# Three edits in an exact-split trunk layer: where the ring's places begin, where two staged operands land, and where two SiLUs stand

## The chip, the cores and the metric

The kernel runs on one core of a Trainium2 chip. The metric is the device time of one execution in microseconds (us). Three runs of the kernel before gave 2100.77, 2100.97 and 2095.59 us, so its median is 2100.77 us. A fourth execution was recorded by the hardware profiler; all rows come from that one.

## The reference

One decoder layer on a sequence of 512 positions with 2048 channels, in float32:

```python
hn = rms_norm(x, norm_mix_pre)
proj = hn @ w_in                       # q | k | v | gate_b | gate_c | hc, 1024 columns each
a = diff_attention(q, k, v, lam, rel_bias)             # 8 heads, causal
a = rms_norm(a, subln_gain) * (1.0 - lambda_init)
c = rms_norm(gate_b * short_conv(gate_c * hc, conv_w), conv_norm_gain)
mix = concat(a, c) @ w_out
x = x + rms_norm(mix, norm_mix_post)
hn = rms_norm(x, norm_ffn_pre)
f = (silu(hn @ w_gate) * (hn @ w_up)) @ w_down         # 5632 hidden columns
out = x + rms_norm(f, norm_ffn_post)
```

## The kernel before

**Products of split operands.** Every large product is made of float32 values that are split in two: ACT copies the value in a reduced type to `hi` (line 99), DVE subtracts that from the value and keeps the rest as `lo` (line 100). A product then takes three matmuls for each slice of 128 rows: hi·hi, hi·lo and lo·hi. These are lines 133, 134 and 135, so nearly all matmuls of the profile stand on those three lines, and the tile names tell the stages apart.

**Stages in order of time.** The v columns of the in-projection (to 113 us, banks `pv`); the q and k columns, the project stage (113 to 272 us, banks `pqk`, moving operands in `t_all` and `acts`); the column jobs of the convolution (to 590 us, banks `pc_h`, `pc_c`, `pc_b`, 512 columns a matmul), with the attention beside them; the out-projection (596 to 775 us, banks `po`, 512 columns); the gate and up projections in quartets (775 to 1648 us, banks `pa`, `pb`, `pd`); the down projection (to about 2060 us, banks `pd`); and the last pieces.

**Quartets.** A quartet q is 256 columns of one of the two FFN matrices: even q are gate, odd q are up, 44 in all. Its product of 2048 × 256 weights by 512 positions is done with seven half-size products in place of eight, in the manner of Strassen, numbered i = 1 to 7. Each is 8 slices × 3 matmuls = 24 matmuls of 256 columns. The weights of a product are sums or differences of blocks made by DVE (`combine`, lines 1015 to 1021) in the raw buffers `raw_q` (gate) or `post` and `pre` (up). The moving operand of products 1, 5, 2 and 3 is in the tensor `acts` (parts `ffn_hi` and `ffn_lo`), that of 7, 6 and 4 in the tiles x0 to x5. Most quartets run their products as 1, 5, 7, 2, 6, 3, 4 (`PLAIN`). The quartets 5, 7, 12 and 24 (`CLOSE`) run them as 1, 2, 5, 7, 6, 3, 4, and `in_turn` issues the first four matmuls of product 5 ahead of product 2.

**The ring.** A product's weights, `hi` and `lo`, stand side by side in one of four places of the tensor `ring_all`, taken in rotation (`ring_tile`). In the program as built `ring_all` begins at byte 196064 of each partition and a place is 8320 bytes behind the one before, so the four begin at bytes 480, 96, 224 and 352 within 512. `acts` begins at byte 416 within 512 and its slices step by 512; the x tiles begin at byte 32. The other stages use the same ring: as weights, or in the down projection and the out-projection as the moving operand.

**The first quartets.** The first four quartets (`HEAD`) run in another order: products (0,1), (1,1), (0,2), (1,2), (2,1), (3,1), (2,2), (3,2), then (0,5), (0,7), (0,3), (0,6), (0,4), then the rest of quartets 1, 2 and 3. Thirteen of their operands (`STAGED`) are split early, written to DRAM (`stg`) and read back by `prepare` through SP's DMA queue: the first two into the buffers with the tag `raw`, of which there are two, the third into `spare`, the others into ring places. At (0,3), seven matmuls of (0,6) are issued ahead. `load_quartet` (line 979) loads the raw weights of later quartets; those of even quartets go to the `raw` buffers.

**Gathering.** `gather` runs behind each product. From quartet 4 on, behind product 1 ACT copies half a bank to `q1` (line 1119), which must come before product 2 may add to that bank. Behind product 4 DVE writes the middle of the result (line 1140) and, in a gate quartet, ACT applies SiLU to the whole 128 × 1024 result (line 1142). `finish` multiplies it with the up quartet's result at the end of the next quartet. Each engine runs its instructions in the order in which they are issued.

Of the kernel before, what the change touches and what calls it, by code (L numbers as in the profile page):

```python
# [12 lines left out]
F32R = mybir.dt.float32r  # L13
AF = mybir.ActivationFunctionType
# [4 lines left out]
P = 128  # L19
D = 2048  # L20
# [35 lines left out]
def trunk(ctx: ExitStack, tc: tile.TileContext, a, out):  # L56
    nc = tc.nc
# [17 lines left out]
    high = ctx.enter_context(tc.tile_pool(name="high", bufs=1, side="right"))  # L75
# [5 lines left out]
        for o in (16, 144 + NT * KC * P, 0, 128 + NT * KC * P)  # L81
    )
    ring = [1]
    ring_all = high.tile([P, 4 * (D + 32)], F32R, name="ring_all")

    def ring_tile(n, m, shift=0):

        i = ring[0] = (ring[0] + 1) % 4
        return ring_all[:, (D + 32) * i + shift :][:, : n * m].rearrange("p (n m) -> p n m", n=n)

    ident = const.tile([P, P], F32, name="ident")
    make_identity(nc, ident)
# [5 lines left out]
    def split(hi, lo, src):  # L98
        first = nc.scalar.copy(hi, src)  # L99
        second = nc.vector.tensor_tensor(out=lo, in0=src, in1=hi.bitcast(F32), op=ALU.subtract)  # L100
        return first.ins, second.ins
# [13 lines left out]
    def ring_parts(raw, n, m):  # L115
        hi = ring_tile(n, m)
        lo = ring_tile(n, m)
        split(hi, lo, raw)
        return hi, lo
# [215 lines left out]
    tmp = {}  # L335
# [432 lines left out]
    def place(tag, dtype=F32, shape=(P, D)):  # L768
        count = late["count"] = late.get("count", 0) + 1
        name = f"{tag}_{count}"  # L770
        return late["mp" if tag[0] == "m" else "fp"].tile(list(shape), dtype, tag=tag, bufs=1, name=name)
# [175 lines left out]
    CLOSE, CLOSE_D = (5, 7, 12, 24), (2,)  # L947
# [9 lines left out]
    def slot(kind):  # L957

        tag, first, width, count = {
            "sg": ("m0", 0, 1024, 2), "s1": ("m1", 0, 1024, 1), "q1": ("m1", 1024, 256, 2), "u": ("m1", 1536, 256, 2),  # L960
            "q57": ("m2", 0, 512, 2), "r": ("m2", 1024, 1024, 1),
        }[kind]
        if ("tmp", tag) not in late:
            late["tmp", tag] = place(tag)
        k = slots[kind] = slots.get(kind, -1) + 1
        o = first + (k % count) * width
        return late["tmp", tag][:, o : o + width]
# [5 lines left out]
    def load_quartet(q):  # L973
        if q % 2 == 0:
            r = [wp.tile([P, 8, 256], F32, tag="raw", name=f"raw_q{q}_{i}") for i in range(2)]
        else:
            r = [place(n, F32, (P, 8, 256)) for n in ("post", "pre")]
        for i in range(2):
            nc.sync.dma_start(r[i], quartet_cols(q)[:, 8 * i : 8 * i + 8, :])
        raws[q] = r  # L980
# [28 lines left out]
    def combine(q, s):  # L1009

        (p11, p21), (p12, p22) = ((r[:, :, :P], r[:, :, P:]) for r in raws[q])
        if s == 1:
            t = slot("s1") if q else place("spare")[:, :1024]
            tmp["s1"] = t.rearrange("p (k m) -> p k m", k=8)
            nc.vector.tensor_add(tmp["s1"], p21, p22)
        elif s == 3:
            nc.vector.tensor_sub(p21, p11, p21)
        elif s == 2:
            nc.vector.tensor_sub(p21, p22, p21)
        else:  # L1020
            nc.vector.tensor_sub(p12, p12, p21)

    def source(q, i):

        if i in (1, 2) and 0 < q < HEAD:
            return heads_raw[q][:, 8 * (i - 1) : 8 * i, :]
        (p11, p21), (p12, p22) = ((r[:, :, :P], r[:, :, P:]) for r in raws[q])
        return {1: p11, 2: p12, 3: p12, 4: p22, 5: tmp.get("s1"), 6: p21, 7: p21}[i]

    def prepare(n):  # L1030

        if n >= len(order):
            return prepare_down(n - len(order))
        q, i = order[n]
        if (q, i) in STAGED:

            if n < 2:
                w = wp.tile([P, 16, P], F32R, tag="raw", name=f"w_{q}_{i}")
            elif n == 2:
                w = place("spare", F32R, (P, 16, P))  # L1040
            else:
                w = ring_tile(16, P)
            nc.sync.dma_start(w.rearrange("p k m -> p (k m)").bitcast(F32), stg[STAGED.index((q, i))])
            operands[n] = w.rearrange("p (a k) m -> p a k m", a=2)
        else:
            src = source(q, i)
            if i == 7 and q >= HEAD:
                combine(q, 3)
            if i == (3 if q == last_q else 6):
                combine(q, 2)  # L1050
            if i == 3:
                combine(q, 4)
            w = ring_tile(16, P).rearrange("p (a k) m -> p a k m", a=2)
            made[q, i] = split(w[:, 0], w[:, 1], src)
            operands[n] = w
        if i == 4:
            if q < last_q - 1:
                load_quartet(q + 2)
            elif q == last_q - 1:
                for j in (0, 1):  # L1060
                    load_block(0, j)
                load_block(0, 2)
            else:
                load_block(0, 3)
# [48 lines left out]
    def gather(n):  # L1113

        q, i = order[n]
        early, (c, up), pq = q < HEAD, quartets[q], psq[q]
        if i == (5 if early else 1):
            tmp["q1", q] = slot("q1")
            nc.scalar.copy(tmp["q1", q], pq["a"][:, :256])  # L1119
        if i == 7:  # L1120
            tmp["r", q] = slot("r") if up else slot("sg")
            if not up:
                tmp["sg", c] = tmp["r", q]
            q57 = tmp["q57", q] = slot("q57")
            nc.scalar.copy(q57, pq["b"])
            nc.vector.tensor_add(tmp["r", q][:, 768:], q57[:, :256], q57[:, 256:])
        if i == 6:
            u = tmp["u", q] = slot("u")
            nc.vector.tensor_add(u, pq["d"][:, 256:], tmp["q1", q])
            nc.vector.tensor_add(tmp["r", q][:, 768:], tmp["r", q][:, 768:], u)  # L1130
            if early:
                nc.vector.tensor_add(tmp["r", q][:, :256], pq["a"][:, 256:], tmp["q1", q])
            else:
                nc.scalar.copy(tmp["r", q][:, :256], pq["a"][:, :256])
        if i != 4:
            return
        u, r = tmp["u", q], tmp["r", q]
        mid = r[:, 256:768].rearrange("p (h n) -> p h n", h=2)
        b = pq["b"].rearrange("p (h n) -> p h n", h=2)
        nc.vector.tensor_tensor(out=mid, in0=b, in1=u[:, None, :].broadcast_to([P, 2, 256]), op=ALU.add)  # L1140
        if not up:
            nc.scalar.activation(r, r, AF.Silu)

# [54 lines left out]
    def load_block(s, j):  # L1200

        g, cb = s // 4, s % 4
        if g > 2:
            return
        if j in (1, 2):
            t = wp.tile([P, 8, 256], F32, tag="raw", name=f"raw_b{s}_{j}")
        else:
            t = place(turns[count_b[0] % 3], F32, (P, 8, 256))
            count_b[0] += 1
        e, half = ((0, 0), (0, 1), (1, 1), (1, 0))[j]  # L1210
        n = FIRST[g + 1] - FIRST[g]
        c0 = cb * 512 + half * 256
        rows = w_down.rearrange("(c e p) m -> p c e m", e=2, p=P)
        nc.sync.dma_start(t[:, :n, :], rows[:, FIRST[g] : FIRST[g + 1], e, c0 : c0 + 256])
        blocks[s, j] = t
# [33 lines left out]
    def prepare_down(n):  # L1249
        if n >= len(steps):  # L1250
            return
        g, cb, i, hf = steps[n]
        s = 4 * g + cb
        ks = pairs(g, hf)
        b11, b12, b22, b21 = (blocks[s, j][:, ks.start : ks.stop, :] if (s, j) in blocks else None for j in range(4))
        if i == 5:
            nc.vector.tensor_sub(b11, b12, b11)
        if i == 7:
            nc.vector.tensor_sub(b12, b22, b12)
        if i == 6:  # L1260
            nc.vector.tensor_sub(b11, b22, b11)
        if i == 4:
            nc.vector.tensor_sub(b21, b21, b11)
        src = {1: b11, 5: b11, 7: b12, 2: b21, 6: b11, 3: b22, 4: b21}[i]
        w = ring_tile(2 * len(ks), 256).rearrange("p (a k) m -> p a k m", a=2)
        made["down"] = split(w[:, 0], w[:, 1], src)
        operands_d[n] = w
        if hf == 1:
            if i == 7:
                load_block(s + 1, 1)  # L1270
            if i == (6 if s in CLOSE_D else 3):
                load_block(s + 1, 2)
            if i == 4:
                load_block(s + 1, 3)
                load_block(s + 2, 0)
# [61 lines left out]
    def ffn(_):  # L1337
        ready, ng = 7, len(order)
        for n in (5, 6):
            prepare(n)  # L1340
# [146 lines left out]
```

## Time and profile before

| | before |
|---|---|
| median of three runs | 2100.77 us (2095.59 to 2100.97) |
| the profiled execution, as a run | 2097.92 us |
| its span, first to last instruction | 2096.1 us |
| mean granted TensorE clock | 0.996 |
| PE busy | 2072.3 us, 99% |
| DVE busy | 1609.6 us, 77% |
| ACT busy | 958.8 us, 46% |
| moved by DMA | 358.57 MB, 171 GB/s on average |

The span is what the profile shows; the run's own time is 1.8 us longer. A row of the timeline has the start in us, the duration in us, the engine, the line, the operation, out<-in with the tile names (buffer numbers left out), and in brackets the idle time of the engine just before and what ended it. A row of groups ends with the count, then the busy time in us and the mean of one in ns, then the idle time before. A row of windows has the stretch, its length, then the busy time (and instructions) of PE, of the weight loads, of DVE, ACT and POOL, then the granted clock, the share of the DMA engines and GB/s; where the view is of SP alone the engines are left out. PE's matmuls overlap, so their rate is read from their starts, not from their durations.

### The profile page before, as it was taken

Reading aid. Unit: us, or ns where it says so; the run is one execution under the profiler, and the core shown is the slowest. Engines: PE = TensorE matmul, PEld = TensorE weight load, DVE = VectorE, ACT = ScalarE, POOL = GpSimd, SP = SyncE. Lnnn points to the kernel's source line nnn. Section 1 sums busy time; section 2 is a strip of 40 time slices with the busy share of each in tenths; the row PEclk is TensorE's granted clock in tenths of the full one; section 3 lists DMA queues with packets and bytes.
Section 4 is the critical chain, followed back from the end, with each engine's and each line's share of the span. In section 5 each row is a group of like instructions: output and inputs, shape, how many; then the busy total and the mean of one; then the engine's idle time right before and its main releaser. Section 6 shows DMA issues by size and latency. Waiting matters only on the chain.

```text
span 2096.1 us, 35907 instructions
## 1 busy us (share of the span) xinstructions
PE 2072.3 (99%) x15180; PEld 1957.8 (93%) x15180; DVE 1609.6 (77%) x2027; ACT 958.8 (46%) x1341; POOL 25.3 (1%) x51
## 2 busy tenths in 40 slices
PE   8999999999999999999999999999999999999998
PEld 6899988888888889999999999999999999999996
DVE  5777747777455478988888889888888777878887
ACT  4344446654334354445445445445544444333442
POOL 0000000000000000000000000000000000000000
PEclk9999999999999999999999999999999999999999
DMA  6444353331239867554544544545545946648354
GB/s 234 137 158 150 112 191 95 98 109 63 92 137 346 293 227 246 176 156 150 158 156 153 161 151 153 163 148 159 160 146 173 331 145 228 230 120 287 106 186 161
DMA packets 301618, 358.57 MB, mean 171 GB/s; under 512 B 11880, under 2 KB 261736, under 8 KB 295568
## 3 DMA queue, kind: packets, MB, share of 16 engines
q1 hardware_dynamic: 299856, 350.48, 50.8%
q10 hardware_dynamic: 1600, 5.79, 0.8%
q8 instruction: 119, 1.95, 0.4%
q14 instruction: 43, 0.35, 0.1%
HBM read 289.11 MB, written 69.75 MB: 171 GB/s over the span
## 4 chain that ended last, share of the span: by engine, by line
PE 92%; DVE 4%; DMA 2%; issue 1%; ACT 1%; SPq 0%; POOL 0%; DVEq 0%; POOLq 0%; ACTq 0%
PE pb L134 7%; PE pb L133 7%; PE pb L135 7%; PE pd L133 6%; PE pd L134 6%; PE pd L135 6%; PE pa L133 5%; PE pa L134 5%; PE pa L135 5%; PE po L134 3%; PE po L133 3%; PE po L135 3%; PE pv L134 1%; PE pv L135 1%; PE pv L133 1%; PE pc_h L135 1%
## 5 line engine op out<-in xcount | busy, mean ns | idle before, releaser
L99 ACT CAST ring_all<-raw_q 128x1024 fp32r<-128x1024 f32 x124 | 130.0, 1050 | 195.2 <-PE pb L134 79.6
L134 PE MATMUL pb<-x,ring_all 128*128 128x256 f32 x704 | 197.2, 280 | 0.0
L135 PE MATMUL pb<-x,ring_all 128*128 128x256 f32 x704 | 197.0, 280 | 0.0
L133 PE MATMUL pb<-x,ring_all 128*128 128x256 f32 x704 | 196.9, 280 | 0.0
L135 PE MATMUL pb<-acts,ring_all 128*128 128x256 f32 x704 | 195.5, 278 | 0.4 <-DVE ring_all L100 0.4
L133 PE MATMUL pb<-acts,ring_all 128*128 128x256 f32 x704 | 195.7, 278 | 0.0
L134 PE MATMUL pb<-acts,ring_all 128*128 128x256 f32 x704 | 195.5, 278 | 0.0
L133 PE MATMUL pa<-acts,ring_all 128*128 128x256 f32 x680 | 190.8, 281 | 2.0 <-ACT m L1119 2.0
L134 PE MATMUL pa<-acts,ring_all 128*128 128x256 f32 x680 | 189.9, 279 | 0.0
L135 PE MATMUL pa<-acts,ring_all 128*128 128x256 f32 x680 | 189.8, 279 | 0.0
L135 PE MATMUL pd<-ring_all,acts 128*128 128x256 f32 x640 | 179.1, 280 | 0.6 <-DMA acts<-hx 0.6
L133 PE MATMUL pd<-ring_all,acts 128*128 128x256 f32 x640 | 179.2, 280 | 0.0
L134 PE MATMUL pd<-ring_all,acts 128*128 128x256 f32 x640 | 179.2, 280 | 0.0
L99 ACT CAST ring_all<-pre 128x1024 fp32r<-128x1024 f32 (+1 forms) x106 | 105.0, 994 | 148.2 <-PE pb L134 78.1
L100 DVE TENSOR_TENSOR ring_all<-raw_q,ring_all 128x1024 fp32r<-128x1024 f32 x124 | 151.2, 1220 | 27.2 <-ACT ring_all L99 26.9
L100 DVE TENSOR_TENSOR ring_all<-pre,ring_all 128x1024 fp32r<-128x1024 f32 (+1 forms) x106 | 122.0, 1153 | 54.4 <-ACT ring_all L99 53.5
L99 ACT CAST ring_all<-post 128x1024 fp32r<-128x1024 f32 (+1 forms) x106 | 105.2, 993 | 102.9 <-PE pd L135 42.4
L100 DVE TENSOR_TENSOR ring_all<-post,ring_all 128x1024 fp32r<-128x1024 f32 (+1 forms) x106 | 121.7, 1148 | 21.7 <-ACT ring_all L99 21.4
L134 PE MATMUL pd<-ring_all,x 128*128 128x256 f32 x480 | 134.6, 280 | 0.2 <-DVE ring_all L100 0.2
L135 PE MATMUL pd<-ring_all,x 128*128 128x256 f32 x480 | 134.4, 280 | 0.0
L133 PE MATMUL pd<-ring_all,x 128*128 128x256 f32 x480 | 134.4, 280 | 0.0
L133 PEld LDWEIGHTS pb<-x,ring_all 128*128 128x128 f32 x704 | 133.3, 189 | 0.0
(343 smaller groups left out, 6515.3 us busy)
## 6 DMA issues: line engine op xcount, KB each, us to landing
raw_q<-in_w_gate SPq DMA_DIRECT2D x42, 1024.0 KB, 5.9
post<-in_w_up SPq DMA_DIRECT2D x22, 1024.0 KB, 5.2
pre<-in_w_up SPq DMA_DIRECT2D x22, 1024.0 KB, 5.1
hx<-spare SPq DMA_DIRECT2D x20, 896.0 KB, 7.8
hx<-m SPq DMA_DIRECT2D x20, 896.0 KB, 8.5
raw_o<-in_w_out SPq DMA_DIRECT2D x16, 1024.0 KB, 7.9
raw_b<-in_w_down SPq DMA_DIRECT2D x16, 896.0 KB, 5.7
acts<-hx SPq DMA_DIRECT2D x32, 448.0 KB, 8.7
```

What stands on the lines that cost most here:

```text
L99: first = nc.scalar.copy(hi, src)
L100: second = nc.vector.tensor_tensor(out=lo, in0=src, in1=hi.bitcast(F32), op=ALU.subtract)
L133: yield nc.tensor.matmul(o, lhsT=lhi, rhs=rhi, start=start, stop=False, **kw).ins
L134: yield nc.tensor.matmul(o, lhsT=lhi, rhs=rlo, start=False, stop=False, **kw).ins
L135: yield nc.tensor.matmul(o, lhsT=llo, rhs=rhi, start=False, stop=stop, **kw).ins
```

## The change

There are three edits. The first changes the stride of the ring from `D + 32` to `D` elements and moves its last two places by 128 elements, 512 bytes. The tensor is 512 bytes larger than before, and it and `acts` begin 512 bytes lower. In the program as built the four places begin at byte 480 within 512, all of them; `acts` (416) and the x tiles (32) keep their bytes within 512. The second sends the staged operands (0,7) and (0,6) to the `raw` buffers in place of ring places. The third issues the SiLU of a gate quartet behind the next quartet's copy to `q1` where the next quartet is in `CLOSE`; of these only 5 and 7 follow a gate quartet, so two SiLUs move, those of quartets 4 and 6.

```diff
-    ring_all = high.tile([P, 4 * (D + 32)], F32R, name="ring_all")
+    ring_all = high.tile([P, 4 * D + 256], F32R, name="ring_all")
...
-        return ring_all[:, (D + 32) * i + shift :][:, : n * m].rearrange("p (n m) -> p n m", n=n)
+        return ring_all[:, D * i + 128 * (i // 2) + shift :][:, : n * m].rearrange("p (n m) -> p n m", n=n)
...
-            if n < 2:
+
+            if n < 2 or (q, i) in ((0, 7), (0, 6)):
                 w = wp.tile([P, 16, P], F32R, tag="raw", name=f"w_{q}_{i}")
...
             tmp["q1", q] = slot("q1")
-            nc.scalar.copy(tmp["q1", q], pq["a"][:, :256])
+            copy = nc.scalar.copy(tmp["q1", q], pq["a"][:, :256])
+            if q in CLOSE and ("silu", q - 1) in tmp:
+                with tc.issue_after(copy.ins):
+                    tmp.pop(("silu", q - 1))()
...
         if not up:
-            nc.scalar.activation(r, r, AF.Silu)
+            silu = lambda: nc.scalar.activation(r, r, AF.Silu)
+            if q + 1 in CLOSE:
+
+                tmp["silu", q] = silu
+            else:
+                silu()
```

The diff moves later lines: the staged load of line 1043 is line 1044 after the change, the copy to `q1` of line 1119 is 1120, and the SiLU of line 1142 is 1146.

On SP's queue, at the staged loads of quartet 0 and the first raw loads of quartet 2, there stands before (`pre` is a raw load of quartet 1; the five loads to the ring are the operands (0,5), (0,7), (0,3), (0,6) and (0,4)):

```order
L979 DMA pre_6628<-in_w_up 128x8x256
L1043 DMA ring_all<-stg 128x2048 x5
L979 DMA raw_q_0_6758<-in_w_gate 128x8x256
L979 DMA raw_q_1_6759<-in_w_gate 128x8x256
L979 DMA post_6934<-in_w_up 128x8x256
```

and after the change:

```order
L979 DMA pre_6628<-in_w_up 128x8x256
L1044 DMA ring_all<-stg 128x2048
L1044 DMA w_7_6665<-stg 128x2048
L1044 DMA ring_all<-stg 128x2048
L1044 DMA w_6_6722<-stg 128x2048
L1044 DMA ring_all<-stg 128x2048
L979 DMA raw_q_0_6760<-in_w_gate 128x8x256
L979 DMA raw_q_1_6761<-in_w_gate 128x8x256
L979 DMA post_6936<-in_w_up 128x8x256
```

The order of the loads is the same; two of them go to the buffers `w_7` and `w_6`, which the two loads to `raw_q_0` and `raw_q_1` take over next. The ring places of all later operands shift by two.

On ACT, at the border between quartets 6 and 7, there stands before (the last copy to m from pa at line 1134 is that of quartet 6; `pa_7949` is the bank of quartet 7):

```order
L1134 COPY m_53_6786<-pa_7739 128x256
L99 CAST ring_all<-m_52_6755 128x1024
L99 CAST ring_all<-post_7651 128x1024
L1142 ACTIVATE m_53_6786<-m_53_6786 128x1024
L1119 COPY m_52_6755<-pa_7949 128x256
L99 CAST ring_all<-post_7651 128x1024
```

and after the change (the bank is `pa_7950`):

```order
L1138 COPY m_53_6788<-pa_7741 128x256
L99 CAST ring_all<-m_52_6757 128x1024
L99 CAST ring_all<-post_7653 128x1024
L1120 COPY m_52_6757<-pa_7950 128x256
L1146 ACTIVATE m_53_6788<-m_53_6788 128x1024
L99 CAST ring_all<-post_7653 128x1024
```

SiLU and copy have changed places, and nothing else moved there. At the border between quartets 4 and 5 the same two are exchanged.

## The prediction

> **What bounds the kernel now.** I read the page first, then the chain, PE's waits, and PE's timeline product by product.
>
> ```profile
> span 2096.1 us, 35907 instructions
> PE 2072.3 (99%) x15180; PEld 1957.8 (93%) x15180; DVE 1609.6 (77%) x2027; ACT 958.8 (46%) x1341; POOL 25.3 (1%) x51
> PE 92%; DVE 4%; DMA 2%; issue 1%; ACT 1%; SPq 0%; POOL 0%; DVEq 0%; POOLq 0%; ACTq 0%
> PE pd L133 <- DMA ring_all<-stg: 2.2, 1, 2.2
> PE pa L133 <- ACT m L1119: 2.0, 1, 2.0
> ```
>
> The matmuls set the end: PE is busy for 99% of the span and carries 92% of the chain. Little waiting is left, and two of the longest single waits are quoted because the change touches both: 2.2 us before a product of quartet 0 whose staged operand arrives late, and 2.0 us in quartet 7 behind the copy of line 1119. So only three things can move the end: these two waits, new waits, and the rate at which PE takes matmuls.
>
> The rate is not one number. The next rows are the first matmuls of successive products in two neighbouring gate/up quartets, 14 and 15; each product is 24 matmuls long and nothing stands between them.
>
> ```profile
> 1059.72 0.28 PE L133 MATMUL pa<-acts,ring_all 128*128 128x256 f32 x1
> 1062.55 0.28 PE L133 MATMUL pb<-acts,ring_all 128*128 128x256 f32 x1
> 1065.27 0.28 PE L133 MATMUL pb<-x,ring_all 128*128 128x256 f32 x1
> 1068.10 0.28 PE L133 MATMUL pa<-acts,ring_all 128*128 128x256 f32 x1
> 1070.84 0.28 PE L133 MATMUL pa<-x,ring_all 128*128 128x256 f32 x1
> 1073.68 0.28 PE L133 MATMUL pb<-acts,ring_all 128*128 128x256 f32 x1
> 1076.42 0.28 PE L133 MATMUL pb<-x,ring_all 128*128 128x256 f32 x1
> 1079.25 0.28 PE L133 MATMUL pa<-acts,ring_all 128*128 128x256 f32 x1
> 1081.99 0.28 PE L133 MATMUL pb<-acts,ring_all 128*128 128x256 f32 x1
> 1084.71 0.28 PE L133 MATMUL pb<-x,ring_all 128*128 128x256 f32 x1
> 1087.54 0.28 PE L133 MATMUL pa<-acts,ring_all 128*128 128x256 f32 x1
> ...
> 1098.85 0.28 PE L133 MATMUL pa<-acts,ring_all 128*128 128x256 f32 x1
> ```
>
> Subtract neighbours. The products of quartet 14 take 2.83, 2.72, 2.83, 2.74, 2.84, 2.74 and 2.83 us; quartet 15 takes 2.74, 2.72, 2.83, and then 11.31 us for its last four, 2.83 each. Same instruction, same shape, two paces: 24 matmuls in 2.73 us (114 ns each) or in 2.83 us (118 ns). Set beside them the ring place that each operand has in the program as built (its first byte within 512). Quartet 14 goes through 96, 224, 352, 480, 96, 224, 352, and quartet 15 through 480, 96, 224, 352, 480, 96, 224. Products whose moving operand is in `acts` (i = 1, 5, 2, 3; the tensor begins at byte 416 and its slices step by 512) are fast at 480 and 224 in four cases of four, and slow at 96 and 352 in three of four. Products that move an x tile (i = 7, 6, 4; byte 32) are slow at all four places. The two quartets last 39.13 us.
>
> The pattern is not that of one pair alone. These are groups of lines 133 and 134 over all quartets from 4 on (863 to 1640 us), and one of the down projection:
>
> ```profile
> L134 PE MATMUL pa<-acts,ring_all 128*128 128x256 f32 x632 | 176.6, 279 | 0.0
> L134 PE MATMUL pb<-acts,ring_all 128*128 128x256 f32 x635 | 176.2, 277 | 0.0
> L133 PE MATMUL pd<-ring_all,acts 128*128 128x256 f32 x640 | 179.2, 280 | 0.0
> ```
>
> A slow matmul lasts 281 ns in the records and a fast one 276. By the pair, i = 1 and 2 (pa) are fast in two cases of four and i = 5 and 3 (pb) in three of four; that would give means of 278.5 and 277.2, and the groups show 279 and 277.
>
> **The change, part by part.** *The places.* Now every place begins at 480, and `acts` and the x tiles keep their bytes. Each `acts` product then stands where it was fast, each x product where it was slow. Of the pair's 14 products, eight go to 2.73 and six stay at 2.83: 38.82 us, 0.31 less. There are 20 pairs from quartet 4 on: **−6.2 us**. The alternative is that the pace follows what ran before rather than the byte: the product at 1081.99 is fast at a slow byte, directly behind a fast one. Bounds: all fast, 39.13 − 14 × 2.73 = 0.91 a pair, −18; all slow, 14 × 2.83 = 39.62, 0.49 a pair, +9.8. I take the byte, for seven `acts` cases of eight and the group means.
>
> The Trainium skill, page "SBUF — State Buffer", section "Who interferes with whom", gives PE two independent read ports, one for the moving operand and one for the weights, and says that PE never waits on anyone. By that no byte of a place can matter and this term would be 0, not −6.2; the rows at 1062.55 (2.72 us) and 1065.27 (2.83 us) show two paces that go with the operands' places, so the trace does not agree, though it does not show why.
>
> The down projection takes its moving operand from the ring; at 280 ns it is nearly all slow although its products pass through all four places, so I take 0 for it. If one in five of its 3360 matmuls is fast now (280 against 281 and 276) and becomes slow, that is +3. The project stage and the stages with 512 columns are next.
>
> ```profile
> L133 PE MATMUL pqk_b<-t_all,ring_all 128*128 128x256 f32 x192 | 53.4, 278 | 0.0
> L133 PE MATMUL pc_b<-acts,ring_all 128*128 128x512 f32 x128 | 51.0, 398 | 0.0
> L133 PE MATMUL po<-ring_all,acts 128*128 128x512 f32 x224 | 88.0, 395 | 0.0
> 739.92 0.39 PE L133 MATMUL po<-x,acts 128*128 128x512 f32 x1
> 743.36 0.39 PE L133 MATMUL po<-x,acts 128*128 128x512 f32 x1
> 751.34 0.40 PE L133 MATMUL po<-x,acts 128*128 128x512 f32 x1
> 756.24 0.40 PE L133 MATMUL po<-x,acts 128*128 128x512 f32 x1
> ```
>
> In the project stage, the three lines of `pqk_b` on `t_all` (576 matmuls) have a mean of 278: all slow +1.7, all fast −1.2. With 512 columns, three matmuls (one of each line) take 0.688 us (five between 739.92 and 743.36) or 0.700 us (seven between 751.34 and 756.24). The column jobs have 3 × 128 such triples and the out-projection 224, so 608 in all; each moves by at most 12 ns, ±7.3, and half of that if they are mixed now, as the means of 395 to 398 suggest. I take 0 for both stages, since the rows do not say which byte is the better one there.
>
> *The SiLU behind the copy.* Quartets 5 and 7 issue four matmuls of product 5 ahead of product 2, so the copy of line 1119 has only those to hide in.
>
> ```profile
> 881.82 0.28 PE L133 MATMUL pb<-acts,ring_all 128*128 128x256 f32 x1
> 882.10 0.38 PE L133 MATMUL pa<-acts,ring_all 128*128 128x256 f32 x1
> 887.40 1.05 ACT L99 CAST ring_all<-post 128x1024 fp32r<-128x1024 f32 x1 [5.35 <-DVE post L1019]
> 921.24 0.28 PE L133 MATMUL pb<-acts,ring_all 128*128 128x256 f32 x1
> 923.49 0.50 PE L133 MATMUL pa<-acts,ring_all 128*128 128x256 f32 x1 [1.97 <-ACT m L1119]
> 922.12 1.06 ACT L1142 ACTIVATE m<-m 128x1024 f32<-128x1024 f32 x1 [2.38 <-DVE m L1140]
> 923.50:927.00 3.50, 3.50 (x17) 3.50 (x18) 3.47 (x4) 1.05 (x1) 0.00 (x0) 0.51 0.18 53
> ```
>
> In quartet 7 the SiLU waits for a sum on DVE until 922.12, and the copy stands behind it although ACT has been idle for 2.38 us. PE pauses 2.25 us between starts (921.24 to 923.49) where quartet 5, whose SiLU was done in time, pauses 0.28: −1.97. Behind the pause the granted clock is 0.51, and 17 matmuls take 3.50 us instead of 17 × 0.118 = 2.0: −1.5. Together **−3.5 us**. Nothing takes the pause's place: behind the copy the SiLU still starts at 922.12. In quartet 5 the copy gains nothing and the SiLU comes about 2 us later, but ACT then sits idle for 5.35 us before its next cast (887.40), which hides 1.06 us. If that cover were gone, the casts behind it would be 1.06 us late: bound +1.
>
> The Trainium skill, page "TensorE: Matmul & The Clock Gate", Part 1, puts the fall to half clock behind an idle window of about 3.4 us. By that a pause of 2.25 us would not cause the 0.51, those 1.5 us could stay and the sum would be 1.5 higher; the trace has the 0.51 right behind the pause, so here it is counted with it.
>
> *The two loads.* Operands 7 and 6 of quartet 0 now go to raw buffers that have long been free, so the load of 6 no longer waits for a ring place.
>
> ```profile
> 808.14 0.36 PE L133 MATMUL pd<-x,ring_all 128*128 128x256 f32 x1 [2.23 <-DMA ring_all<-stg]
> 804.00:807.00 3.00, 1.00 0.87 300
> raw_q<-in_w_gate SPq DMA_DIRECT2D x42, 1024.0 KB, 5.9
> raw_q<-in_w_gate SPq DMA_DIRECT2D x2, 1024.0 KB, 12.5
> 819.98 1.21 DVE L1015 TENSOR_TENSOR m<-raw_q,raw_q 128x1024 f32<-128x1024 f32 x1
> ```
>
> Product 6 waits 2.23 us for it. But the DMA engines are near full there (0.87 busy at 300 GB/s in the stretch that ends at the landing), and the bytes ahead of it in the queue are the same, so an earlier issue mostly makes it stand longer in the queue. What can be filled is 0.13 × 3.00: **−0.4 us**; bounds 0 and −2.2. In exchange quartet 2's two raw loads, next on SP's queue, wait for these buffers, the second until product 6 ends. Product 6 issues 7 matmuls, then product 3 its 24, then product 6 the rest: 48 × 0.118 = 5.7 us behind 808.14, so 813.8. With 5.9 us to landing it is there at 819.7, and DVE first needs it at 819.98: hidden, with 0.3 us to spare. I take 0. The two loads themselves took 12.5 us when they stood behind the staged ones; with that the second would come at 826.3, 6 us late, and DVE would be late by as much with everything queued behind: bound +6.
>
> **The sum.** −6.2 − 3.5 − 0.4 = −10.1. The profiled execution took 2097.92 us as a run, so 2087.8. It lies 2.9 below the median of the three runs (2100.77), which themselves reach from 2095.59 to 2100.97; the four have a mean of 2098.8, 0.9 above it, and with this I say **2088.7 us**.
>
> **The rivals.** *The byte decides nothing for the pace.* Against it stand seven of eight cases; for it stands that x products are slow at all places and that 1081.99 does not fit. Then −3.9 alone: 2098.8 − 3.9 = 2094.9. The rule quoted above from the Trainium skill (page "SBUF — State Buffer") would give this too.
>
> *The pace has a memory and locks slow.* x products, three in seven, are always slow, and four slow products in a row run at the end of quartet 15, an `acts` product on 352 and one on 96 among them. Today it is the change of place between products that brings the fast pace back (1065.27 to 1068.10 changes 352 for 480). With one byte for all, that trigger is gone; if it is needed, all products are slow: +9.8 in the quartets, +1.7 in the project stage, less 3.9: 2106.4.
>
> *Slower than before: the same lock in the 512-wide stages too.* The mechanism is the last one, its place the column jobs and the out-projection as well as the quartets; its price 2106.4 plus half of 7.3, so 2110. It becomes slower than before once the pace lost exceeds the 3.9 that the waits give, which is when two fifths of the 9.8 come.
>
> *The edit of the loads or of the SiLU does not do what it says* (the load lands no earlier, the copy finds ACT busy with something else): 2088.7 plus 0.4 or 3.5, 2089 to 2092, inside the first case's range.
>
> **How the numbers follow.** The forecast has 0.46, the byte without effect 0.28, the slow lock in the quartets 0.18, and in all stages 0.08. About 0.3% is what a measurement of this kernel can tell from no change: faster means below 2094.5, slower above 2107.1. The first case is faster but for 0.03; the second lies on the border, half and half; the third is half same, half slower with the bounds of the other stages (half, because +3 on the down projection or part of the +6 of quartet 2's loads carries it over); the fourth is slower but for 0.02. That gives 0.57 faster, 0.28 same, 0.15 slower. The range leaves out the fourth case, the upper edge of the third, and gains beyond 7 us in the unpriced stages: 2081 to 2107. The forecast's own range is 2083 to 2094.
>
> **What would show it.** In the profile after, each step has its row. The places: `acts` products in the gate/up quartets take 2.73 us and x products 2.83, and the groups of pa and pb on `acts` both have a mean of 276 to 277; a mean of 280 to 281 is the lock. The SiLU: no row of L1120 among PE's waits and a clock of 1.00 at that place. The loads: PE's wait for `stg` loads becomes one on a `w` tile, about 1.8 us long, and no new wait stands in quartet 2. The prediction is wrong if the pace in the down projection or the 512-wide stages moves by more than its bounds, or if x products become fast as well.

## The result, and the profile after

The changed kernel takes 2068.72 us, the median of four runs (2066.94 to 2071.81), against 2100.03 us for the kernel before on the same chip (four runs). The ratio is 0.9857 with a 95% interval of 0.9837 to 0.9876: 1.4% faster, some 30 us. The forecast was 2088.7 us with a range from 2081 to 2107. The direction was right, and the gain is three times the forecast's.

The page of the profile after, its first lines and the chain:

```profile
span 2070.0 us, 35911 instructions
PE 2046.8 (99%) x15180; PEld 1936.9 (94%) x15180; DVE 1607.4 (78%) x2027; ACT 958.6 (46%) x1341; POOL 26.0 (1%) x51
PE 89%; DVE 4%; DMA 4%; issue 1%; ACT 1%; POOL 0%; SPq 0%; DVEq 0%; POOLq 0%; ACTq 0%
```

PE's busy time fell by 25.5 us and the span by 26.1 us. So, on balance, nearly nothing of the gain is a wait that went: the same 15180 matmuls run faster. (The span's gain is smaller than that of the medians, because the profiled execution of after, 2071.81 us, is the slowest of its four runs.)

Where they run faster can be read from the first matmul of each stage in the two profiles:

| first matmul of | before, us | after, us | gained in the stage ahead of it, us |
|---|---|---|---|
| the project stage | 115.80 | 114.79 | 1.0 (v columns) |
| the column jobs | 272.37 | 273.09 | −1.7 (project) |
| the out-projection | 590.76 | 587.76 | 3.7 (columns) |
| quartet 0 | 775.24 | 770.36 | 1.9 (out-projection) |
| quartet 4 | 859.21 | 854.76 | −0.4 (quartets 0 to 3) |
| quartet 8 | 941.61 | 933.37 | 3.8 (with quartet 7's wait) |
| the down projection | 1646.67 | 1632.93 | 5.5 (quartets 8 to 43) |
| the last pieces | 2043.32 | 2017.21 | 12.4 (down projection) |

The largest step is the down projection, which the forecast had at 0. Two of its groups of after:

```profile
L134 PE MATMUL pd<-ring_all,acts 128*128 128x256 f32 x640 | 176.8, 276 | 0.0
L134 PE MATMUL pd<-ring_all,x 128*128 128x256 f32 x480 | 132.7, 277 | 0.3 <-DVE ring_all L100 0.3
```

Both had a mean of 280 before: the down projection went over from the slow pace to the fast one. The quartets did what the forecast said. Quartet 14 in the timeline of after, the first matmul of each product, and that of quartet 15:

```profile
1051.25 0.28 PE L133 MATMUL pa<-acts,ring_all 128*128 128x256 f32 x1
1053.98 0.28 PE L133 MATMUL pb<-acts,ring_all 128*128 128x256 f32 x1
1056.70 0.28 PE L133 MATMUL pb<-x,ring_all 128*128 128x256 f32 x1
1059.53 0.28 PE L133 MATMUL pa<-acts,ring_all 128*128 128x256 f32 x1
1062.25 0.28 PE L133 MATMUL pa<-x,ring_all 128*128 128x256 f32 x1
1065.08 0.28 PE L133 MATMUL pb<-acts,ring_all 128*128 128x256 f32 x1
1067.81 0.28 PE L133 MATMUL pb<-x,ring_all 128*128 128x256 f32 x1
1070.63 0.28 PE L133 MATMUL pa<-acts,ring_all 128*128 128x256 f32 x1
...
1090.01 0.28 PE L133 MATMUL pa<-acts,ring_all 128*128 128x256 f32 x1
```

All four `acts` products take 2.72 to 2.73 us, all three x products 2.82 to 2.83; the pair of quartets takes 38.76 us (forecast 38.82, before 39.13).

The waits of PE after, those that the change touches:

```profile
PE pd L135 <- DVE ring_all L100: 1.6, 2, 1.2
...
PE pd L133 <- DMA w<-stg: 0.4, 1, 0.4
...
PE pa L133 <- ACT m L1120: 0.3, 1, 0.3
```

The wait for product 6 of quartet 0 fell from 2.23 to 0.36 us; two waits of DVE's, 1.6 us together, are new. They are in quartets 2 and 3, and the timeline shows what they hang on (DVE first, then PE):

```profile
815.41 1.23 DVE L1015 TENSOR_TENSOR m<-raw_q,raw_q 128x1024 f32<-128x1024 f32 x1 [2.82 <-DMA raw_q<-in_w_gate]
```

```profile
801.82 0.36 PE L133 MATMUL pd<-x,w 128*128 128x256 f32 x1 [0.36 <-DMA w<-stg]
...
830.59 0.39 PE L135 MATMUL pd<-x,ring_all 128*128 128x256 f32 x1 [0.40 <-DVE ring_all L100]
...
846.41 0.38 PE L135 MATMUL pd<-x,ring_all 128*128 128x256 f32 x1 [1.21 <-DVE ring_all L100]
```

DVE stood still for 2.82 us until quartet 2's raw weights came, and its operands for quartets 2 and 3 were late by 0.40 and 1.21 us. The border between quartets 6 and 7, on ACT and in a window of all engines:

```profile
916.63 0.37 ACT L1120 COPY m<-pa 128x256 f32<-128x256 f32 x1 [1.08 <-PE pa L135]
917.93 1.06 ACT L1146 ACTIVATE m<-m 128x1024 f32<-128x1024 f32 x1 [0.93 <-DVE m L1144]
```

```profile
915.50:919.00 3.50, 3.49 (x31) 3.29 (x30) 3.47 (x5) 1.48 (x3) 0.00 (x0) 1.00 1.15 345
```

The copy now follows PE at once, and PE runs through: 31 matmuls in 3.5 us at a clock of 1.00.

### The profile page after: what moved, and what is told of

Read it like the earlier page. It is cut to its first block, busy times and chain, and to the rows that moved or that the text cites. A ratio compares the mean times of both kernels' runs of the same rounds, so it can differ in the third digit from the quotient of the medians.

```text
span 2070.0 us, 35911 instructions
## 1 busy us (share of the span) xinstructions
PE 2046.8 (99%) x15180; PEld 1936.9 (94%) x15180; DVE 1607.4 (78%) x2027; ACT 958.6 (46%) x1341; POOL 26.0 (1%) x51
## 4 chain that ended last, share of the span: by engine, by line
PE 89%; DVE 4%; DMA 4%; issue 1%; ACT 1%; POOL 0%; SPq 0%; DVEq 0%; POOLq 0%; ACTq 0%
PE pb L134 6%; PE pd L135 6%; PE pb L133 6%; PE pd L134 6%; PE pb L135 6%; PE pd L133 6%; PE pa L133 5%; PE pa L134 5%; PE pa L135 5%; PE po L135 3%; PE po L133 3%; PE po L134 3%; DVE ring_all L100 2%; DMA raw_q<-in_w_gate 2%; PE pv L134 1%; PE pqk_b L133 1%
## 5 line engine op out<-in xcount | busy, mean ns | idle before, releaser
L134 PE MATMUL pb<-x,ring_all 128*128 128x256 f32 x696 | 194.8, 280 | 0.0
L135 PE MATMUL pb<-x,ring_all 128*128 128x256 f32 x696 | 194.3, 279 | 0.5 <-DVE ring_all L100 0.5
L133 PE MATMUL pb<-x,ring_all 128*128 128x256 f32 x696 | 194.2, 279 | 0.0
L133 PE MATMUL pd<-ring_all,acts 128*128 128x256 f32 x640 | 176.9, 276 | 0.7 <-DMA acts<-hx 0.7
L135 PE MATMUL pd<-ring_all,acts 128*128 128x256 f32 x640 | 176.9, 276 | 0.7 <-DMA acts<-hx 0.7
L134 PE MATMUL pd<-ring_all,acts 128*128 128x256 f32 x640 | 176.8, 276 | 0.0
L134 PE MATMUL pd<-ring_all,x 128*128 128x256 f32 x480 | 132.7, 277 | 0.3 <-DVE ring_all L100 0.3
L133 PE MATMUL pd<-ring_all,x 128*128 128x256 f32 x480 | 132.6, 276 | 0.0
L135 PE MATMUL pd<-ring_all,x 128*128 128x256 f32 x480 | 132.6, 276 | 0.0
L135 PEld LDWEIGHTS pb<-acts,ring_all 128*128 128x128 f32 x704 | 132.3, 188 | 0.0
```

The source lines that it names most:

```text
L133: yield nc.tensor.matmul(o, lhsT=lhi, rhs=rhi, start=start, stop=False, **kw).ins
L134: yield nc.tensor.matmul(o, lhsT=lhi, rhs=rlo, start=False, stop=False, **kw).ins
L135: yield nc.tensor.matmul(o, lhsT=llo, rhs=rhi, start=False, stop=stop, **kw).ins
```

## The experiments

In all of them "fast" and "slow" mean the two paces of the 256-column matmuls, 276 and 281 ns in the groups. "Distance" is the weights' first byte less the moving operand's, within 256. Ratios are to the kernel before on the same chip, with the 95% interval.

### Which edit, and which property of the ring (e1 to e4)

**e1**: the ring edit alone.

```diff
-    ring_all = high.tile([P, 4 * (D + 32)], F32R, name="ring_all")
+    ring_all = high.tile([P, 4 * D + 256], F32R, name="ring_all")
...
-        return ring_all[:, (D + 32) * i + shift :][:, : n * m].rearrange("p (n m) -> p n m", n=n)
+        return ring_all[:, D * i + 128 * (i // 2) + shift :][:, : n * m].rearrange("p (n m) -> p n m", n=n)
```

> The kernel before with the ring edit alone. Theory C (what counts is the change of the places' byte from operand to operand; with one byte for all the pace is kept): nearly the whole gain, about -24 us against before, with the down projection's groups at 276 ns and the 2.0-us and 2.2-us waits of before still there. Theory R (the loads or the SiLU have a large indirect effect, or their two skipped ring places decide the pace): under half of the 31 us.

Measured: 2071.62 us, ratio 0.9872 (0.9855 to 0.9888). Its waits still have 2.7 us at line 1119 and 1.4 us for `stg`. The ring alone brings nearly all of it.

**e2**: the change with the old ring, so the two loads and the SiLUs alone (the edit is e1's, reversed, in the changed kernel).

> The changed kernel with the old ring, so the loads and the SiLUs alone. Theory C: -2 to -6 us against before (3.5 us for quartet 7, 1.9 us for the wait before product 6 of quartet 0, less about 2 us of new waits in quartets 2 and 3), the down projection's groups stay at 280 ns. Theory R: more than -15 us.

Measured: 2094.77 us, ratio 0.9988 (0.9979 to 0.9998); one of its ten runs took 9596 us for a cause that nothing here shows, the others lie between 2093.45 and 2098.22. That is −3.0 us, within theory C's bounds; the forecast had −3.9 for these two edits. The new waits are there too (1.8 us in its profile), so they belong to the loads, not to the ring.

**e3**: the changed kernel, with the down projection's operands on four different bytes again.

```diff
-        w = ring_tile(2 * len(ks), 256).rearrange("p (a k) m -> p a k m", a=2)
+        w = ring_tile(2 * len(ks), 256, shift=32 * ((ring[0] + 1) % 4)).rearrange("p (a k) m -> p a k m", a=2)
```

> The changed kernel, but the down projection's operands stand at the four old bytes within 512 (480, 96, 224, 352) in turn; all else as after. Theory C: the down projection loses its 12.4 us again, so about +12 us against after, its groups of pd back at 280 ns, and the gate/up quartets stay as after. Theory A (it was the lower address of acts and ring, 512 bytes, that made the down projection fast): no more than 2 us slower than after. Theory P (each product's pace follows its own byte): a quarter of the products, those on 480, stay fast, +9 us.

Measured: 2083.20 us, ratio 0.9934 (0.9916 to 0.9951), 14.5 us above after. In its profile the down projection takes 400.2 us, where before has 396.7 and after 384.3. Its groups of line 134:

```profile
L134 PE MATMUL pd<-ring_all,acts 128*128 128x256 f32 x640 | 179.9, 281 | 0.0
L134 PE MATMUL pd<-ring_all,x 128*128 128x256 f32 x480 | 134.6, 280 | 0.2 <-DVE ring_all L100 0.2
```

The whole down projection is slow again, the operands at byte 480 included. Theory C (the change of byte costs) holds; that a byte is good for itself (P) and that the lower address of `acts` did it (A) fall.

**e4**: the kernel before with `[P, 4 * (D + 32) + 128]`, which moves `acts` and the ring to the addresses of after without changing the places' bytes.

> The kernel before with 512 bytes of padding behind the ring, so that acts and ring begin 512 bytes lower as after, but the four places keep their four bytes within 512. Theory C: as before, within 3 us. Theory A: at least -12 us, the down projection at 276 ns.

Measured: 2098.00 us, ratio 1.0003 (0.9994 to 1.0013), the down projection at 280 ns. Theory A falls a second time.

### Which byte, and with which period (e5 to e8)

All four are the changed kernel with another offset of place i in `ring_tile` (the rest of the line stays as it is):

```diff
-        return ring_all[:, D * i + 128 * (i // 2) + shift :][:, : n * m].rearrange("p (n m) -> p n m", n=n)
+        return ring_all[:, D * i + 128 * (i // 2) + 64 + shift :]              # e5
+        return ring_all[:, D * i + 128 * (i // 2) + 32 + shift :]              # e6
+        return ring_all[:, D * i + shift :]                                    # e7
+        return ring_all[:, D * i + 128 * (i // 2) + 64 * (i % 2) + shift :]    # e8
```

> The changed kernel with all four places 256 bytes further on, at byte 224 within 512. Theory C (the change of byte from operand to operand is what costs): within 3 us of after, the down projection at 276 ns. Theory B (480 is a good byte for itself): more than 8 us slower than after, the down projection at 280 ns again.

Measured: 2069.46 us, ratio 0.9865 (0.9846 to 0.9883), the down projection at 276 ns, as after.

> The changed kernel with all four places 128 bytes further on, at byte 96 within 512, where the acts products of the quartets were mostly slow before. Theory C alone: the down projection stays at 276 ns and the kernel is within 3 us of after. Theory B: acts products in the quartets at 281 ns, about +9 us for them, and the down projection at 280 ns, +12 us, so about +20 us. Both in part (the down projection only needs one byte, the quartets need the right one): about +9 us.

Measured: 2085.94 us, ratio 0.9933 (0.9906 to 0.9960). Groups of line 134:

```profile
L134 PE MATMUL pb<-acts,ring_all 128*128 128x256 f32 x704 | 196.7, 279 | 0.0
...
L134 PE MATMUL pd<-ring_all,acts 128*128 128x256 f32 x640 | 176.7, 276 | 0.0
...
L134 PE MATMUL pqk_b<-t_all,ring_all 128*128 128x256 f32 x192 | 53.0, 276 | 0.0
```

The down projection stays fast although the byte is one of those that were slow before; in the quartets, `acts` products turn slow (279 against 276 after). The third of the expectations, "both in part", was asked for +9 us and the run is 17 us above after: the direction and the two signs in the groups are right, the size is not. The 512-wide stages lost their gain too (the out-projection begins at 591.25 us, after 587.76).

> The changed kernel without the 512 bytes ahead of the last two places, so that all four places are also alike within 1024. Theory C: within 2 us of after. Theory M (what counts is the byte within 1024): a change of at least 5 us in the down projection or the quartets, faster or slower.

Measured: 2068.02 us, ratio 0.9855 (0.9839 to 0.9871). The 512 bytes ahead of the last two places do nothing that could be seen.

> The changed kernel with places at 480 and 224 within 512 in turn, the two bytes at which acts products were fast before. Theory C with a period of 512: each operand changes the byte, the down projection is back at 280 ns, about +12 us or more against after. With a period of 256: within 3 us of after. Theory B for the quartets: acts products stay at 276 ns whatever the down projection does.

Measured: 2070.36 us, ratio 0.9867 (0.9851 to 0.9882), the down projection's two groups at 277 and 276 ns. Places that differ by 256 count as alike; places that differ by 128 (e3) do not. So for the down projection it isn't which byte, but that the byte within 256 stays the same from operand to operand; for the quartets it must also be the right one, 224 and not 96.

### The loads (e9)

**e9**: the changed kernel with `if n < 2:` in place of `if n < 2 or (q, i) in ((0, 7), (0, 6)):`.

> The changed kernel with the two staged loads back in the ring; ring and SiLUs as after. Theory L (the loads gain their 1.9-us wait and lose about as much again in quartets 2 and 3, whose raw loads come later): within 1 us of after. Theory G (the waits in quartets 2 and 3 of after's profile are an accident of that execution): 2 us slower than after.

Measured: 2070.29 us, ratio 0.9869 (0.9856 to 0.9881) against 0.9857 (0.9837 to 0.9876) of after. The medians differ by 1.6 us and the intervals overlap, so these runs do not tell what the loads bring from nothing. In the profiles quartets 0 to 3 take 82.6 us without the loads (e9) and 84.4 with them (after), but also 81.8 (e5) and 86.2 (e3) with the same instructions there, so one profile cannot settle it either.

### What keeps a pace (e10 to e15)

**e10**: the changed kernel with the x tiles 128 bytes further on, so that x products have the same bytes as `acts` products.

```diff
         late["fp"] = ctx.enter_context(tc.tile_pool(name="ffn", bufs=1))
+        late["fp"].tile([P, 32], F32, tag="pad", bufs=1, name="pad")
```

> The changed kernel with 128 bytes of padding ahead of the FFN tiles, so that the x tiles begin at byte 160 within 512 and weights lie 64 bytes behind the moving operand within 256 in x products as in acts products. Theory D (the distance within 256 between weights and moving operand decides, 64 is a fast one): x products in the quartets at 276 ns instead of 280, about -12 us against after. Theory X (x products are slow for another reason, their tile's layout): within 2 us of after.

Measured: six runs from 2060.21 to 2090.00 us, median 2068.97, ratio 0.9880 (0.9837 to 0.9923). The median says nothing here; the spread of 30 us does, since no other kernel of this study but e12 and e14 has one above 10 (the run of e2 at 9596 us apart). The groups of its profiled execution (2061.73 us), first from 917 to 1014 us and then from 1016 to 1640 us:

```profile
L134 PE MATMUL pb<-acts,ring_all 128*128 128x256 f32 x80 | 22.5, 281 | 0.0
...
L134 PE MATMUL pb<-x,ring_all 128*128 128x256 f32 x80 | 22.5, 281 | 0.0
```

```profile
L134 PE MATMUL pb<-x,ring_all 128*128 128x256 f32 x512 | 141.3, 276 | 0.0
L134 PE MATMUL pb<-acts,ring_all 128*128 128x256 f32 x511 | 141.0, 276 | 0.0
```

Once no byte changes, x and `acts` products share one pace, and it is slow without exception for five quartets and then fast for thirty-two. The x products are no slow kind (theory X falls), and a distance of 64 isn't always fast (theory D falls as it stood).

**e11**: the changed kernel with `ring_tile(16, P, 48)` in place of `ring_tile(16, P, 16)` in the project stage.

> The changed kernel with the project stage's operands 128 bytes further on in their ring places, so that they lie 64 bytes behind t_all within 256 (and 192 behind acts). Theory D: the pqk groups on t_all go from 279-280 to 276 ns, 768 matmuls by 4.5 ns, -3.5 us; the groups on acts stay at 280. Theory X: no change.

Measured: 2069.95 us, ratio 0.9864 (0.9850 to 0.9878); `pqk_b` on `t_all` has a mean of 281 ns at line 134. A miss: no gain, although in e6, with the same bytes for these products, the same group had 276.

**e12**: the edits of e10 and e11 together.

> The last two edits together. Theory D: about -15 us against after, 2053 us. Theory X: as after.

Measured: five runs from 2054.61 to 2069.22 us, median 2061.38, ratio 0.9832 (0.9811 to 0.9852). The median lies between the two theories, and one run came near theory D's 2053. Groups of its profiled execution (2068.41 us) from 1013 to 1249 us, and from 1251 to 1626 us:

```profile
L134 PE MATMUL pb<-acts,ring_all 128*128 128x256 f32 x192 | 54.0, 281 | 0.0
```

```profile
L134 PE MATMUL pb<-acts,ring_all 128*128 128x256 f32 x319 | 88.0, 276 | 0.0
```

In the timeline its pace turns at 877, 916, 1012 and 1250 us: in quartets 5, 7, 12 and 24, where four matmuls of product 5 go ahead of product 2, and nowhere else between quartets 5 and 43. In e10 it turns in 5, 7 and 12 and not in 24. The order is not the only thing that is special there. Product 2 also starts late, as the last of these turns shows:

```profile
1249.00 0.28 PE L133 MATMUL pb<-acts,ring_all 128*128 128x256 f32 x1
1249.27 0.38 PE L133 MATMUL pa<-acts,ring_all 128*128 128x256 f32 x1
```

Its start is 0.27 us behind the one before, not 0.11. All seven turns of e10 and e12 between quartets 5 and 43 stand at such a pause of 0.27 to 0.28 us. The way back, from product 2 to the rest of product 5, changes the order once more but has no pause, and the pace never turns there.

**e13**: e10, with product 4's weights 128 bytes further on and the places 256 bytes further on one by one.

```diff
-        return ring_all[:, D * i + 128 * (i // 2) + shift :][:, : n * m].rearrange("p (n m) -> p n m", n=n)
+        return ring_all[:, (D + 64) * i + shift :][:, : n * m].rearrange("p (n m) -> p n m", n=n)
...
-            w = ring_tile(16, P).rearrange("p (a k) m -> p a k m", a=2)
+            w = ring_tile(16, P, 32 if i == 4 else 0).rearrange("p (a k) m -> p a k m", a=2)
```

> e10 (x tiles moved by 128 bytes), but from quartet 4 on the weights of product 4, the last of each quartet, stand 128 bytes further on in their place (the places now begin 256 bytes further on one by one, which e8 showed to be alike). Theory K (a pace is kept until the distance between weights and moving operand changes; going from 192 back to 64 within 256 brings the fast one): in each quartet products 1, 5, 7, 2, 6 and 3 are fast again, whatever the pace was; runs lie within 5 us of each other, 6 to 10 us faster than after (2059 to 2063). Theory D (distance 64 is always fast): as e10 at its best, 2060, plus 4 us. Theory Z (the pace is an accident): a spread of over 15 us as in e10.

Measured: 2056.99 us (2053.77 to 2058.72), ratio 0.9802 (0.9789 to 0.9815). This beats both kernels: 2.0% below before, some 12 us below after, with a spread of 5 us. Groups from 962 to 1615 us:

```profile
L134 PE MATMUL pb<-acts,ring_all 128*128 128x256 f32 x552 | 152.6, 276 | 0.0
L134 PE MATMUL pb<-x,ring_all 128*128 128x256 f32 x546 | 150.9, 276 | 0.0
```

Its profile shows once how a pace is lost and comes back, in quartet 6, with nothing out of order (the border between products 6 and 3, then that between product 4 and quartet 7's product 1):

```profile
904.29 0.28 PE L135 MATMUL pa<-x,ring_all 128*128 128x256 f32 x1
904.54 0.39 PE L133 MATMUL pb<-acts,ring_all 128*128 128x256 f32 x1
...
910.07 0.28 PE L134 MATMUL pb<-x,ring_all 128*128 128x256 f32 x1
910.18 0.28 PE L135 MATMUL pb<-x,ring_all 128*128 128x256 f32 x1
910.30 0.28 PE L133 MATMUL pa<-acts,ring_all 128*128 128x256 f32 x1
910.41 0.28 PE L134 MATMUL pa<-acts,ring_all 128*128 128x256 f32 x1
```

Product 3 starts 0.25 us behind the matmul ahead of it, and products 3 and 4 run slow; product 1 of quartet 7, back at a distance of 64, is fast from its first matmul. That is theory K's return. It is seen once, and two pauses in quartet 9 (0.86 and 0.56 us) turned the pace to slow and back without any change of distance; the pauses of 0.28 us in quartets 5, 7, 12 and 24 left it fast. For the return in every quartet speaks the spread of 5 us in four runs where e10's six have 30. The theory was wrong in one thing: product 4, at a distance of 192, keeps the fast pace as well, which fits a run faster than the 2059 to 2063 expected.

**e14**: e10 with `CLOSE, CLOSE_D = (), (2,)`.

> e10, but no quartet issues four matmuls of product 5 ahead of product 2 (all quartets run in the plain order), and no SiLU moves. Theory K: nothing between quartets 4 and 43 changes a distance or interrupts the order, so the pace hardly changes there: the profile shows one pace over most of the stretch, and runs fall into some near 2055 and some near 2085 us. Theory Z: pace changes within that stretch are as many as in e10, at other places.

Measured: eight runs from 2078.03 to 2096.26 us, median 2084.49, ratio 0.9945 (0.9922 to 0.9969). Groups of its profiled execution from 852 to 1646 us:

```profile
L134 PE MATMUL pb<-x,ring_all 128*128 128x256 f32 x647 | 182.1, 281 | 0.0
L134 PE MATMUL pb<-acts,ring_all 128*128 128x256 f32 x641 | 180.4, 281 | 0.0
L134 PE MATMUL pa<-acts,ring_all 128*128 128x256 f32 x640 | 180.1, 281 | 0.0
```

Without the quartets that interrupt the order nothing turns the pace for 794 us: 40 quartets in the slow one. Their pauses are gone with them: no two starts of this stretch are more than 0.12 us apart, so this run alone cannot tell order from pause (e13's quartet 6 can). One pace over the whole stretch is what theory K said; that some runs would be near 2055 us did not come in eight. The bytes are those of e10, which was fast for most of that stretch.

**e15**: the changed kernel with places as in e13 and `32 if i in (4, 6, 7) else 0` as the shift, x tiles where they were.

> The changed kernel with the x tiles where they were, but from quartet 4 on the weights of the x products (7, 6, 4) 128 bytes further on in their places, so that weights lie 64 bytes behind the moving operand in all products, and both bytes change together. Theory D: x products at 276 ns, 10 to 12 us faster than after. Theory K with weights and moving operand apart (any change of the moving byte within 256 ends the fast pace): x products stay at 280 or 281 ns, within 3 us of after, and acts products may lose their pace too, up to +9 us.

Measured: 2070.04 us, ratio 0.9866 (0.9854 to 0.9879). Groups from 860 to 1630 us:

```profile
L134 PE MATMUL pb<-x,ring_all 128*128 128x256 f32 x629 | 177.1, 282 | 0.0
...
L134 PE MATMUL pb<-acts,ring_all 128*128 128x256 f32 x632 | 175.0, 277 | 0.0
```

The distance is 64 in all products, and x products are slow nevertheless: at each step to them the moving operand's byte changes by 128. The `acts` products are fast although the distance never changes, so the step back of both bytes brings the pace back too; theory K's change of distance isn't needed for it.

## Why the prediction was wrong, step by step

**The quartets: right.** The forecast put `acts` products at 2.73 us and x products at 2.83, 38.82 us a pair; the pair shown takes 38.76, and the 18 pairs from quartet 8 on gain 5.5 us, 0.31 each, so 20 pairs come to 6.1 where −6.2 was said.

**The down projection: the step that failed.** The prediction took 0 "since it is nearly all slow although its products pass through all four places". From that it read that its pace doesn't depend on the ring. But passing through the four places was itself the cause. There the ring holds the moving operand, and before the change its byte moved by 128 with every operand. e3 gives that back and loses the gain; e5, e6 and e8 hold the byte at 224, at 96 and at two values 256 apart, and the groups stay at 276 and 277 ns. The rows that would have warned are in the prediction: it had noticed that the product at 1081.99 is fast at a "slow" byte directly behind a fast one, and that going from one place to another brings a pace back. It made this memory a rival that locks slow; all fast was only a bound for the quartets (−18), and for this stage +3 and 0 bounded the wrong side. This step alone is 12.4 of the 20.0 us between the forecast of 2088.7 and the 2068.72 measured, and the forecast's range left out gains beyond 7 us in the unpriced stages.

**The 512-wide stages: mis-sized.** 0 was taken, with 7.3 us as the bound; the columns gained 3.7 us, the out-projection 1.9 and the v columns, which had no term, 1.0. The project stage lost 1.7, its bound.

**The SiLU: right.** −3.5 was said; the stretch from quartet 4 to quartet 8 gains 3.8, of which the ring has 0.6 (two pairs), so 3.2 are left. e1 and e9 differ in this edit alone and take 82.9 and 79.5 us for this stretch, 3.5 apart. Pause and half clock are both gone; e1 and e4, without the edit, pause 2.7 us at that place and have 3.4 us at half clock behind it.

**The loads: the sum was near, both of its parts were not.** The wait for product 6 fell by 1.87 us, not 0.4: the DMA engines' share of 0.87 was no measure of what an earlier issue gains. And the 0.3 us said to be left for quartet 2's raw loads were not left: DVE stood 2.82 us, and PE pays 1.6 us in quartets 2 and 3. In the one profile of after the two nearly cancel. In the profiles of other kernels with the two loads these waits of `pd` at line 135 come to between 0.2 us (e5) and 2.4 us (e3), and in those without (e1, e4, e9) there are none, so they go with the loads and vary in size; e9 cannot tell the rest from zero.

**The rivals.** That the byte decides nothing, and that the pace locks slow, were both wrong for this change. A slow pace that stays exists, though: e14 shows it.

## What to carry to other kernels

A stream of matmuls that waits for nothing can still have two rates 4% apart, so read the starts of a stage's matmuls and compare neighbours of the same shape before calling PE busy "at its limit". When a resource is slow at every one of several settings that it passes through in turn, that doesn't show that the setting is indifferent: hold it still once. And when a tuned kernel's runs spread by about a per cent or more (e10, e14), look for a state that is kept, and give it a place where it is set again in each round (e13), rather than choosing by the median.

## What the runs showed of the hardware

Two paces of a 128 × 256 matmul on split float32 operands, 2.72 and 2.83 us for 24 of them, depend on the bytes at which weights and moving operand begin. A moving byte that changes by 128 from operand to operand costs 12 us in the down projection of before and 16 in that of e3 (some 1 us of it longer waits), both against after; 256 cost nothing (e8). Other steps than 128, 256 and 512 were not tried in it.

The pace is kept from product to product, and three things were seen to move it. Going from `acts` to an x tile, with the moving byte changing by 128, ended the fast pace, both where the distance goes from 64 to 192 (after) and where it stays at 64 (e15). Going back to `acts` at a distance of 64 brought it back in nearly every quartet of both. At a distance of 192 it did not: `acts` products in e6 are slow. And a pause between two starts turned the pace either way, though not each time: 0.27 to 0.28 us in e10 and e12, 0.25 to 0.86 us in e13. With none of these it stayed the same for 794 us (e14).

Three things stay open: what in the chip makes the two paces; why a pause turns the pace at some times and not at others; and why the project stage is fast on `t_all` in e6 (276 ns) and slow in e11 (281 ns) with the same bytes in those products, the v columns ahead of it being all that differs before it.

The Trainium skill, page "SBUF — State Buffer", section "Who interferes with whom", has PE wait on nobody at its two read ports. By that e3 and after would run the down projection alike; their groups at line 134 have means of 281 and 276 ns on `acts`, so these runs do not agree with it as far as the operands' bytes go.
